# One step of a hybrid sparse-attention and linear-attention trunk: the order of the first loads, splits and products is changed

## The chip, the cores and the metric

The kernel runs on one core of one Trainium2 chip. The metric is device microseconds of one execution. Times of the kernel before are the median of three runs; the profile is of a further execution, taken by the hardware profiler.

The engines are called as in the profile: PE is TensorE (PEld its weight loads), DVE is VectorE, ACT is ScalarE, POOL is GpSimd, SP is SyncE, which issues most of the transfers (DMA).

## What is computed

One inference step of a decoder layer for 1024 prompt tokens and 64 sample tokens (8 sequences of 8 tokens). All 1088 tokens pass through the same weights:

```python
z = split_projection(x @ w_in)          # 13 parts: q_a, k_a, v_a, q_i, k_i, w_i, q_b, k_b, v_b, g_b, a_b, gate_a, gate_b
attn = attend(q_a, k_a, v_a, q_i, k_i, w_i)      # branch A
# log-decay from a_b, chunked gated linear attention over q_b, k_b, v_b  -> o_b   # branch B
merged = sigmoid(gate_a) * (attn @ w_attn_o) + sigmoid(gate_b) * (o_b @ w_gla_o)
mix = merged @ w_out
h = layer_norm(ALPHA * x + mix)
y = layer_norm(ALPHA * h + square(relu(h @ w_ff1)) @ w_ff2)
```

Branch A chooses for every query the 256 keys with the highest indexer score, which is the sum over 8 heads of w_i times relu(q_i . k_i), and attends to those alone. The prompt's keys are its own tokens; a sample's keys are 4096 cached ones, found through a page table, and its own 8 tokens. The model width is 1024, the hidden width 4096.

## The kernel before, in words

**Layout.** Activations stand feature-major: x is eight tiles of 128 features by 1088 tokens. Tokens are cut into three chunks, `CH` (line 36): 384, 384 and 320. Every operand of a large product is split into two parts of type fp32r, a rounded high part and the rest (for x: `xh` and `xl`; for weights: `wh` and `wl`), and a product is three matmuls for each of the eight blocks of 128 inputs: high by high, high by low, low by high (`mm3`, line 620; `fmajor`, line 629, for one weight tile and one token chunk). So one weight tile and one chunk take 24 matmuls, one weight tile and all tokens 72. The matmuls write to one of eight banks; ACT and DVE read the bank.

**Two builds and a planner.** The kernel is built twice. In the first build the uses of every buffer are counted. In the second, a model of the engines' times (class `Clock`, line 97, with a cost for every instruction and a landing time for every transfer) decides in which order the instructions are issued: work is written as generators ("streams", line 262), each of which yields what it has to wait for, and `Order.run` (line 299) takes the first stream in its list whose operands are ready by the model. On the chip each engine executes its own list in exactly this order and waits at an instruction whose operands aren't there. PE's list is common to all streams. The planner also decides whether DVE or POOL makes a low part (`sub`, line 406).

**Jobs.** The stream `main` (line 1701) goes through a list of jobs, one weight tile each. Job 0 is misc (its 128 columns hold k_i, w_i and a_b), job 1 qi0, the first of four tiles with two of the eight q_i heads each; then come the other qi tiles, ka, va, qa, the projections of branch B, the gates, and after them the products with w_attn_o, w_gla_o and w_out. The second half of the kernel (`back`) holds the MLP. `w_get(i)` (line 451) hands out the weight tile of job i, and sees to it that the tile of the next job is split (`w_split`, line 440: ACT makes the high part, DVE or POOL the low part) and that the one behind that is loaded (`w_load`, line 430).

**The start.** SP first issues the loads of the page table, spread over all partitions (`ptab`, line 424), and of a small table of page rows (`ptg`, line 426); then the weight of misc in one load of 0.5 MB (line 468); then x, chunk by chunk, in loads of two feature blocks (line 476), with the weight of qi0 behind the first chunk (line 478). POOL makes the identity matrix `idf` (line 361). DVE works out the row numbers for the gather of cached indexer keys, `ix_i` from ptg and `ix_k` from ptab (lines 496 to 499). Then ACT and DVE split x (lines 533 to 538: an activation and a subtraction for each feature block and chunk); between the first and the second block of the first chunk stands the split of misc's weight (line 540).

**misc and qi0.** `misc_job` (line 668) multiplies the three chunks in turn. After each, ACT copies the whole result to `misc`, and ACT and DVE write the parts that other streams use (`kkh`, `kkl`: the indexer keys; `as3`: the decay input). Behind the third chunk, k_i goes to the output `kidxT` through SP (line 682). `qi_job` (line 658) multiplies its three chunks and splits them into stacks (`to_stacks`, line 645). The stream `wtok_job` (line 687) waits until misc is done, and turns w_i with eight small transposes (`pw`); the streams of the indexer start behind it. `idx_sample` has one more small product there (`pww`).

**What else is named below.** `pages_in_order` (line 514) takes gathered cache rows (`cig`, 16 gathers by POOL) and stores them to DRAM (`ci_s`), from where `idx_sample` loads them again (`kir`) when the gathers are through and the indexer of the prompt has come to its last head. The streams `top_first`, `top_second` and `top_sample` search the threshold of the 256th key bit by bit; a step of `top_sample` (line 1047) is two counts on ACT (`jka`), a small product on PE that adds them for pairs of partitions (`ppr`), and three small operations on DVE (`gs_m`, `gs_u`, `gs_f`). Behind the other two searches DVE makes the masks (`fin`, line 955).

Of the kernel before, what the change touches and what calls it, by code (L numbers as in the profile page):

```python
# [12 lines left out]
F32 = mybir.dt.float32  # L13
F32R = mybir.dt.float32r
# [3 lines left out]
AF = mybir.ActivationFunctionType  # L18
OP = mybir.AluOpType
# [4 lines left out]
P = 128  # L24
# [3 lines left out]
KT = 8  # L28
# [7 lines left out]
CH = ((0, 384), (384, 384), (768, 320))  # L36
# [42 lines left out]
M_SC = 1.0  # L79
M_SD = 0.5  # L80
NGATE = 4
WLATE = 4.0


def f32(ap):
    return ap.bitcast(F32)


def view(ap, offset, dims):
    return bass.AP(tensor=ap.tensor, offset=ap.offset + offset, ap=[list(d) for d in dims])  # L90
# [6 lines left out]
class Clock:  # L97
# [67 lines left out]
    def bank(self, tile):  # L165
        name = tile.tensor.name
        self.psum.add(name)
        free = [i for i in range(8) if self.banks[i] is None or self.banks[i] not in self.pinned]
        i = min(free, key=lambda i: self.used.get(self.banks[i], 0.0))
        self.after[name] = self.used.get(self.banks[i], 0.0)  # L170
        self.banks[i] = name
# [203 lines left out]
def front(ph, tc, env, A, O):  # L375
    nc = tc.nc
    clock = env["clock"]
    pe, dve, act, pool, sp = env["eng"]
    bank, unpin, const, idf = env["bank"], env["unpin"], env["const"], env["idf"]
# [9 lines left out]
    def page(name, dt=F32, shape=None):  # L389
        return clock.take(pgs.tile(shape or [P, T], dt, name=name, tag="pg", bufs=NPG), name, "pg", NPG)  # L390
# [30 lines left out]


    ptab = page("ptab", I32, [P, 8, 32])
    sp.dma_start(ptab, view(A["page_table"], 0, [[0, P], [32, 8], [1, 32]]))
    ptg = cst("ptg", [P, 2], I32)
    sp.dma_start(ptg, A["page_rows"])
    jobs = []
    wt = {}

    def w_load(i):  # L430
        src, kt, m = jobs[i][0]
        pages = []
        for k0 in range(0, kt, 1024 // m):
            kn = min(1024 // m, kt - k0)
            r = page(f"wr{i}_{k0}", F32, [P, kn, m])
            sp.dma_start(r, src[:, k0:k0 + kn, :])
            pages.append([r, None, kn])
        wt[i] = pages

    def w_split(i):  # L440
        for n, e in enumerate(wt[i]):
            r = e[0]
            h = page(f"wh{i}_{n}", F32R, list(r.shape))
            l = page(f"wl{i}_{n}", F32R, list(r.shape))
            act.activation(h, r, AF.Copy)
            sub(l, r, f32(h), WLATE if 1 < state["job"] < mix_at - 1 else 0.0)
            e[0], e[1] = h, l

    state = {"dma": 0, "split": 0, "job": 0}

    def w_get(i):
        while state["split"] <= min(i + (i not in env["alone"]), len(jobs) - 1):
            while state["dma"] <= min(state["split"] + (1 if i < env["deep"] else 2), len(jobs) - 1):
                w_load(state["dma"])
                state["dma"] += 1
            w_split(state["split"])
            state["split"] += 1
        hs, ls = [], []
        for h, l, kn in wt.pop(i):
            for k in range(kn):  # L460
                hs.append(h[:, k, :])
                ls.append(l[:, k, :])
        return hs, ls
# [2 lines left out]
    jobs.append([(W1[4], 8, P), None, None])  # L466
    jobs.append([(W1[0], 8, P), None, None])
    w_load(0)
    state["dma"] = 1
    xh = [env["xpage"](f"xh{k}", F32R, (P, T)) for k in range(KT)]  # L470
    xl = [page(f"xl{k}", F32R) for k in range(KT)]
    xr = {}
    for c, (c0, n) in enumerate(CH):
        for k in range(0, KT, 2):
            xr[k, c] = page(f"xr{k}{c}", F32, [P, 2, 384])
            sp.dma_start(xr[k, c][:, :, :n], A["xT"][k:k + 2, :, c0:c0 + n].rearrange("k p t -> p k t"))
        if c == 0:
            w_load(1)
            state["dma"] = 2


    pid = const("pid", [P, 1], I32)
# [10 lines left out]


    ix_i = cst("ix_i", [P, 8, 2], I32)
    for g in range(8):
        dve.tensor_scalar(ix_i[:, g], ptg, 8.0, float(g), op0=OP.mult, op1=OP.add)
    ix_k = const("ix_k", [1, 256], I32)
    dve.tensor_scalar(ix_k, ptab[0:1].rearrange("p a b -> p (a b)"), 128.0, None, op0=OP.mult)

# [27 lines left out]
                     view(ci_s[p // 2], (p % 2 * 64 + qq * 16) * 8192, [[P, P], [16384, 8], [1, P]]))  # L530


    for c, (c0, n) in enumerate(CH):
        for k in range(KT):
            s = slice(c0, c0 + n)
            r = xr[k - k % 2, c][:, k % 2, :n]
            act.activation(xh[k][:, s], r, AF.Copy)
            dve.tensor_sub(xl[k][:, s], r, f32(xh[k][:, s]))
            if c == 0 and k == 0:
                w_split(0)  # L540
                state["split"] = 1

    def iota_f(name, shape, pattern, base=0):
        n = int(np.prod(shape))
# [84 lines left out]
    def fmajor(w, c, name):  # L629

        c0, n = CH[c]
        ps = bank(name, True)
        yield from mm3(ps[:, :n], w[0], w[1], [x[:, c0:c0 + n] for x in xh], [x[:, c0:c0 + n] for x in xl])
        unpin(ps)
        return ps
# [9 lines left out]
    def to_stacks(ps, c, st):  # L645

        c0, n = CH[c]
        for e in range(2):
            own, oth = slice(e * 64, e * 64 + 64), slice(64 - e * 64, 128 - e * 64)
            act.activation(st[e][own, c0:c0 + n], ps[own, :n], AF.Copy)  # L650
        for e in range(2):
            own, oth = slice(e * 64, e * 64 + 64), slice(64 - e * 64, 128 - e * 64)
            dve.tensor_sub(st[e][oth, c0:c0 + n], ps[own, :n], f32(st[e][own, c0:c0 + n]))

    qis = {}
# [10 lines left out]
        return run  # L666

    def misc_job(w):
        for c in range(3):
            c0, n = CH[c]  # L670
            ps = yield from fmajor(w, c, f"misc{c}")
            act.activation(misc[:, c0:c0 + n], ps[:, :n], AF.Copy)
            for e in range(2):
                act.activation(kkh[e * 64:e * 64 + 64, c0:c0 + n], ps[0:64, :n], AF.Copy)
            for r in (64, 32):
                act.activation(as3[r:r + 16, c0:c0 + n], ps[64:80, :n], AF.Copy)
            for e in range(2):
                dve.tensor_sub(kkl[e * 64:e * 64 + 64, c0:c0 + n], ps[0:64, :n], f32(kkh[0:64, c0:c0 + n]))
            dve.tensor_sub(as3[0:16, c0:c0 + n], ps[64:80, :n], f32(as3[64:80, c0:c0 + n]))
        act.activation(kkn[:, 0], f32(kkh[:, TP:T]), AF.Copy)  # L680
        act.activation(kkn[:, 1], f32(kkl[:, TP:T]), AF.Copy)
        sp.dma_start(O["kidxT"], misc[0:64])
        flags.add("misc")

    flags = set()
# [1015 lines left out]
    def main():  # L1701
        for i in range(len(jobs)):
            state["job"] = i
            if i == project_at - 1:
                x_load(0)
            if i == mix_at - BLEAD:
                gp_load(0)
                branch_load(0)
                gp_load(1)
                branch_load(1)  # L1710
            if jobs[i][2]:
                yield jobs[i][2]
            yield from jobs[i][1](w_get(i))
        while late:
            late.popleft()()

# [739 lines left out]
```

## Time and profile before

| | us |
|---|---|
| median of three runs | 2098.71 (2098.24 to 2099.25) |
| the profiled execution | 2093.24 |
| its span | 2091.5 |
| PE busy | 2032.9 (97%) |
| PEld busy | 1958.7 (94%) |
| DVE busy | 1263.2 (60%) |
| ACT busy | 1120.0 (54%) |
| POOL busy | 761.5 (36%) |

The mean granted clock of PE is 0.988 of full speed, and the transfers move 264.50 MB, 126 GB/s in the mean. A line of the order of time begins with start and length in us; at its end, in square brackets, stands how long the engine had been idle before it, and what ended that. Nearly all instructions are issued through a helper, so that they have one line number (256); they are told apart by the names of their tiles, output first: `misc<-xh,wh` is a matmul that writes a bank of misc from the high parts of x and the weight. A view of waits gives, for each pair of waiting and releasing work, the microseconds in total, the number of times and the longest. A view by stretches gives for each stretch its length, then busy time and number of instructions of PE, PEld, DVE, ACT and POOL, the mean granted clock, the busy share of the DMA engines and GB/s.

### The profile page before, as it was taken

Reading aid. Unit: us, or ns where it says so; the run is one execution under the profiler, and the core shown is the slowest. Engines: PE = TensorE matmul, PEld = TensorE weight load, DVE = VectorE, ACT = ScalarE, POOL = GpSimd, SP = SyncE. Lnnn points to the kernel's source line nnn. Section 1 sums busy time; section 2 is a strip of 40 time slices with the busy share of each in tenths; the row PEclk is TensorE's granted clock in tenths of the full one; section 3 lists DMA queues with packets and bytes.
Section 4 is the critical chain, followed back from the end, with each engine's and each line's share of the span. In section 5 each row is a group of like instructions: output and inputs, shape, how many; then the busy total and the mean of one; then the engine's idle time right before and its main releaser. Section 6 shows DMA issues by size and latency. Waiting matters only on the chain.

```text
span 2091.5 us, 34541 instructions
## 1 busy us (share of the span) xinstructions
PE 2032.9 (97%) x12423; PEld 1958.7 (94%) x12423; DVE 1263.2 (60%) x2633; ACT 1120.0 (54%) x2220; POOL 761.5 (36%) x567
## 2 busy tenths in 40 slices
PE   7999999999799999999999999999999999999997
PEld 7989999898789999989999899999999999999996
DVE  6977777756845675753167755566554444466635
ACT  5687767787567755673024334445343232445543
POOL 3244121222321113113044335565655343364452
PEclk9999999999899999999999999999999999999998
DMA  7674311212023224255573234655523443145542
GB/s 243 254 210 119 124 29 56 82 48 78 27 81 115 83 84 155 68 160 171 190 258 124 69 103 138 182 167 146 159 91 107 124 139 100 61 136 163 186 149 79
DMA packets 185595, 264.50 MB, mean 126 GB/s; under 512 B 22208, under 2 KB 119488, under 8 KB 185424
## 3 DMA queue, kind: packets, MB, share of 16 engines
q1 hardware_dynamic: 177872, 236.87, 35.0%
q0 software_dynamic: 7552, 25.43, 3.9%
q8 instruction: 98, 1.61, 0.3%
q14 instruction: 73, 0.60, 0.1%
HBM read 212.72 MB, written 49.51 MB: 125 GB/s over the span
## 4 chain that ended last, share of the span: by engine, by line
PE 89%; DVE 4%; issue 3%; ACT 2%; POOL 1%; DMA 1%; SPq 0%; ACTq 0%; POOLq 0%; DVEq 0%
PE pf L256 33%; PE gate L256 9%; PE gb L256 4%; PE pwo L256 4%; PE psv L256 4%; PE pmb L256 4%; PE qb L256 2%; PE kb L256 2%; PE qi L256 2%; PE psc L256 2%; PE qa L256 2%; PE po L256 2%; PE pma L256 2%; PE psq L256 2%; PE pov L256 2%
## 5 line engine op out<-in xcount | busy, mean ns | idle before, releaser
L256 PE MATMUL pf<-a,w 128*128 128x384 f32 (+1 forms) x2304 | 397.9, 329 | 2.2 <-POOL a L256 1.3
L256 PE MATMUL pf<-h,w 128*128 128x384 f32 (+1 forms) x2304 | 394.0, 327 | 3.0 <-POOL w L256 1.7
L256 PEld LDWEIGHTS pf<-a,w 128*128 128x128 f32 x2304 | 379.1, 188 | 6.5 <-POOL a L256 1.8
L256 PEld LDWEIGHTS pf<-h,w 128*128 128x128 f32 x2304 | 378.5, 188 | 5.6 <-POOL w L256 2.1
L256 POOL TENSOR_TENSOR wl<-wr,wh 128x1024 fp32r<-128x1024 f32 (+1 forms) x66 | 150.3, 2279 | 467.9 <-ACT wh L256 412.8
L256 POOL TENSOR_TENSOR w<-wr,w 128x512 fp32r<-128x512 f32 x137 | 195.1, 1432 | 132.3 <-ACT w L256 122.2
L256 ACT ACTIVATE w<-wr 128x512 fp32r<-128x512 f32 x272 | 156.5, 618 | 62.7 <-PE pf L256 26.4
L256 DVE TENSOR_TENSOR w<-wr,w 128x512 fp32r<-128x512 f32 x135 | 140.6, 1051 | 52.7 <-ACT w L256 50.2
L256 DVE TENSOR_TENSOR acc<-acc,pf 128x384 f32<-128x384 f32 (+1 forms) x136 | 72.9, 538 | 99.1 <-PE pf L256 98.8
L256 PE MATMUL gate<-xh,wh 128*128 128x384 f32 (+1 forms) x384 | 129.9, 338 | 0.0
L256 PE MATMUL gate<-xh,wl 128*128 128x384 f32 (+1 forms) x384 | 125.5, 327 | 0.0
L256 PE MATMUL gate<-xl,wh 128*128 128x384 f32 (+1 forms) x384 | 125.5, 327 | 0.0
L256 POOL TENSOR_TENSOR a<-fr,a 128x384 fp32r<-128x384 f32 (+1 forms) x54 | 52.6, 975 | 194.5 <-ACT a L256 190.3
L256 ACT ACTIVATE wh<-wr 128x1024 fp32r<-128x1024 f32 (+1 forms) x75 | 74.4, 1005 | 76.2 <-DMA wr<-wgo 39.2
L256 ACT ACTIVATE fr<-pf 128x384 f32<-128x384 f32 (+1 forms) x96 | 44.9, 467 | 113.6 <-PE pf L256 112.6
L256 DVE TENSOR_TENSOR fr<-fr,pf 128x384 f32<-128x384 f32 (+1 forms) x96 | 50.8, 529 | 90.7 <-ACT fr L256 90.5
L256 ACT ACTIVATE a<-fr 128x384 fp32r<-128x384 f32 (+1 forms) x96 | 48.7, 507 | 81.1 <-DVE fr L256 81.1
L256 DVE TENSOR_SCALAR_CACHE_REDUCE jk<-sc,ga_f 128x1024 int8<-128x1024 f32 (+2 forms) x96 | 88.4, 921 | 2.1
L256 ACT ACTIVATE jkb<-sc,gb_f 128x896 int8<-128x896 f32 (+2 forms) x96 | 86.0, 896 | 4.3 <-DVE gb_f L256 2.7
L256 DVE TENSOR_TENSOR phl<-ppt,phl 128x512 fp32r<-128x512 f32 (+1 forms) x80 | 50.2, 636 | 60.4 <-ACT phl L256 59.9
L256 PE MATMUL psv<-wh,xh 128*128 128x256 f32 (+1 forms) x288 | 83.9, 291 | 0.0
L256 PE MATMUL psv<-wl,xh 128*128 128x256 f32 (+1 forms) x288 | 81.2, 282 | 0.0
(487 smaller groups left out, 5158.1 us busy)
## 6 DMA issues: line engine op xcount, KB each, us to landing
wr<-wff SPq DMA_DIRECT2D x256, 256.0 KB
wr<-w SPq DMA_DIRECT2D x43, 512.0 KB
ckr<-kT SPq DMA_DIRECT2D x256, 64.0 KB
ga_s<-gate SPq DMA_DIRECT2D x16, 544.0 KB
ci_s<-cig SPq DMA_DIRECT2D x16, 512.0 KB
kir<-ci_s SPq DMA_DIRECT2D x16, 512.0 KB
wr<-wout SPq DMA_DIRECT2D x13, 512.0 KB
mgp<-ga_s SPq DMA_DIRECT2D x16, 384.0 KB
```

Source lines behind the costliest of these rows:

```text
L256: r = f(*a, **k)
```

## The change

It concerns the first loads, the splits of the first two weights and of x, and the order of the first two jobs.

- The weight of misc is loaded first, in two halves, each ahead of a piece of x's first chunk; the weight of qi0 follows the first chunk as before; ptg comes behind that, and ptab behind all of x.
- 28 transposes of the identity into a bank that nobody reads are put at the head of PE's list.
- The two halves of misc's weight are split by ACT and DVE ahead of the feature blocks 0 and 4 of the first chunk; qi0's weight is split by ACT and DVE behind the first chunk, and `ix_i` is worked out there; `ix_k` comes behind all splits of x.
- `misc_job` multiplies misc and qi0 in the order misc chunk 0, qi0 chunk 0, misc chunk 1, qi0 chunk 1, misc chunk 2, qi0 chunk 2; `main` passes over job 1. The output kidxT is sent ahead of qi0's last chunk; the flag for which `wtok_job` waits is set behind it. `w_get(1)`, which loads the weights of the next two jobs and splits the first of them, is called behind qi0's first chunk.

```diff
@@ front @@
     ptab = page("ptab", I32, [P, 8, 32])
-    sp.dma_start(ptab, view(A["page_table"], 0, [[0, P], [32, 8], [1, 32]]))
     ptg = cst("ptg", [P, 2], I32)
-    sp.dma_start(ptg, A["page_rows"])
@@ w_load @@
-            sp.dma_start(r, src[:, k0:k0 + kn, :])
+            if i > 1:
+                sp.dma_start(r, src[:, k0:k0 + kn, :])
@@ front @@
     w_load(0)
-    state["dma"] = 1
+    w_load(1)
+    state["dma"] = 2
...
-    for c, (c0, n) in enumerate(CH):
+    w0, src0 = wt[0][0][0], jobs[0][0][0]
+
+    def x_in(k, c):
+        c0, n = CH[c]
+        xr[k, c] = page(f"xr{k}{c}", F32, [P, 2, 384])
+        sp.dma_start(xr[k, c][:, :, :n], A["xT"][k:k + 2, :, c0:c0 + n].rearrange("k p t -> p k t"))
+
+    for k in range(0, KT, 2):
+        if k < 4:
+            sp.dma_start(w0[:, 2 * k:2 * k + 4], src0[:, 2 * k:2 * k + 4, :])
+        x_in(k, 0)
+    sp.dma_start(wt[1][0][0], jobs[1][0][0])
+    sp.dma_start(ptg, A["page_rows"])
+    for c in (1, 2):
         for k in range(0, KT, 2):
-            xr[k, c] = page(f"xr{k}{c}", F32, [P, 2, 384])
-            sp.dma_start(xr[k, c][:, :, :n], A["xT"][k:k + 2, :, c0:c0 + n].rearrange("k p t -> p k t"))
-        if c == 0:
-            w_load(1)
-            state["dma"] = 2
+            x_in(k, c)
+    sp.dma_start(ptab, view(A["page_table"], 0, [[0, P], [32, 8], [1, 32]]))
...
-    for g in range(8):
-        dve.tensor_scalar(ix_i[:, g], ptg, 8.0, float(g), op0=OP.mult, op1=OP.add)
     ix_k = const("ix_k", [1, 256], I32)
-    dve.tensor_scalar(ix_k, ptab[0:1].rearrange("p a b -> p (a b)"), 128.0, None, op0=OP.mult)
...
+    def halves(i):
+        r = wt[i][0][0]
+        h = page(f"wh{i}_0", F32R, list(r.shape))
+        l = page(f"wl{i}_0", F32R, list(r.shape))
+        wt[i][0][:2] = h, l
+        return h, l, r
+
+    warm = bank("warm")
+    for _ in range(WARM):
+        pe.transpose(warm[:, :P], idf, idf)
+    wtop, wnext = halves(0), halves(1)
     for c, (c0, n) in enumerate(CH):
         for k in range(KT):
+            if c == 0 and k in (0, 4):
+                h, l, r = (x[:, k:k + 4] for x in wtop)
+                act.activation(h, r, AF.Copy)
+                dve.tensor_sub(l, r, f32(h))
             s = slice(c0, c0 + n)
             r = xr[k - k % 2, c][:, k % 2, :n]
             act.activation(xh[k][:, s], r, AF.Copy)
             dve.tensor_sub(xl[k][:, s], r, f32(xh[k][:, s]))
-            if c == 0 and k == 0:
-                w_split(0)
-                state["split"] = 1
+        if c == 0:
+            h, l, r = wnext
+            act.activation(h, r, AF.Copy)
+            dve.tensor_sub(l, r, f32(h))
+            for g in range(8):
+                dve.tensor_scalar(ix_i[:, g], ptg, 8.0, float(g), op0=OP.mult, op1=OP.add)
+    dve.tensor_scalar(ix_k, ptab[0:1].rearrange("p a b -> p (a b)"), 128.0, None, op0=OP.mult)
+    state["split"] = 2
@@ misc_job @@
     def misc_job(w):
+        (h, l, kn), = wt[1]
+        q = [h[:, k, :] for k in range(kn)], [l[:, k, :] for k in range(kn)]
+        st = [page(f"qi{e}", F32R) for e in range(2)]
         for c in range(3):
             c0, n = CH[c]
+            if c:
+                ps = yield from fmajor(q, c - 1, f"qi0_{c - 1}")
+                to_stacks(ps, c - 1, st)
+            if c == 1:
+                w_get(1)
             ps = yield from fmajor(w, c, f"misc{c}")
...
         sp.dma_start(O["kidxT"], misc[0:64])
+        ps = yield from fmajor(q, 2, "qi0_2")
+        to_stacks(ps, 2, st)
+        qis.update(enumerate(st))
         flags.add("misc")
@@ main @@
-            yield from jobs[i][1](w_get(i))
+            if i != 1:
+                yield from jobs[i][1](w_get(i))
```

`WARM` is 28.

More of the change, by code (lines that the diff above doesn't have):

```diff
@@ L81 @@
 NGATE = 4
+WARM = 28
 WLATE = 4.0
```

## The prediction

> **What bounds the kernel now.** I read the page's head first, then TensorE's waits, then the order of time of the first 45 us.
>
> ```profile
> span 2091.5 us, 34541 instructions
> PE 2032.9 (97%) x12423; PEld 1958.7 (94%) x12423; DVE 1263.2 (60%) x2633; ACT 1120.0 (54%) x2220; POOL 761.5 (36%) x567
> ```
>
> TensorE (PE) is busy 97% of the span: its work decides the time, and what can be gained without removing products are the 58.6 us (2091.5 - 2032.9) in which it stands, and stretches in which its products run slowly. All but a few of the changed lines act before 45 us. There PE's waits are:
>
> ```profile
> PE misc L256 <- ACT wh L256: 9.0, 1, 9.0
> PE misc L256 <- POOL wl L256: 1.4, 1, 1.4
> PE pw L256 <- ACT misc L256: 1.4, 1, 1.4
> PE qi L256 <- DVE wl L256: 1.1, 1, 1.1
> ```
>
> In the order of time (start, length, engine, operation) the same stretch reads:
>
> ```profile
> 0.82 0.40 SPq L256 DMA_DIRECT2D ptab<-page_table  x1
> 1.74 0.44 SPq L256 DMA_DIRECT2D wr<-w  x1
> 2.22 2.11 SPq L256 DMA_DIRECT2D xr<-xT  x4
> 7.51 0.52 ACT L256 ACTIVATE xh<-xr 128x384 fp32r<-128x384 f32 x1 [5.41 <-DMA xr<-xT]
> 7.94 1.04 ACT L256 ACTIVATE wh<-wr 128x1024 fp32r<-128x1024 f32 x1
> 9.04 0.69 PE L256 MATMUL misc<-xh,wh 128*128 128x384 f32 x1 [9.04 <-ACT wh L256]
> 9.07 2.36 POOL L256 TENSOR_TENSOR wl<-wr,wh 128x1024 fp32r<-128x1024 f32 x1 [7.59 <-ACT wh L256]
> 11.96 0.52 PE L256 MATMUL misc<-xh,wh 128*128 128x384 f32 x1
> ...
> 15.44 0.34 PE L256 MATMUL misc<-xh,wl 128*128 128x384 f32 x1
> ...
> 21.33 0.31 PE L256 MATMUL misc<-xh,wh 128*128 128x320 f32 x1
> ...
> 24.84 0.34 PE L256 MATMUL qi<-xh,wh 128*128 128x384 f32 x1
> 25.14 1.22 DVE L256 TENSOR_TENSOR wl<-wr,wh 128x1024 fp32r<-128x1024 f32 x1
> 29.99 0.52 PE L256 MATMUL qi<-xl,wh 128*128 128x384 f32 x1
> ...
> 42.30 0.34 PE L256 MATMUL qi<-xh,wh 128*128 128x384 f32 x1
> ```
>
> Two things are to be seen. First, the waits: PE begins at 9.04, when the weight's high part is there, and stands again for its low part, which GpSimd (POOL) needs 2.36 us for. Second, the pace. From 15.44 to 21.33 34 products of 384 columns start, 0.173 us each; from 21.33 to 24.84 24 of 320 columns, 0.146 us each. But from 11.96 to 15.44 it is 11 of 384 columns, 0.316 us each, and the product at 29.99 has the same length of 0.52 us as these, against 0.34. The view by stretches (busy us of PE, its weight loads, DVE, ACT, POOL, then the granted clock) has the reason for the latter:
>
> ```profile
> 25.00:30.00 5.00, 2.59 (x17) 1.91 (x16) 4.26 (x8) 4.84 (x12) 0.00 (x0) 0.90 0.01 2
> 30.00:35.00 5.00, 5.00 (x23) 4.68 (x23) 2.83 (x6) 2.46 (x6) 1.87 (x1) 0.76 0.93 300
> ```
>
> The granted clock is 0.90 and 0.76 there, where PE was busy for only 2.59 of the first 5 us. At half the clock that makes 1.0 and 2.4 us (0.10 and 0.24 of 5, twice), and half of these 3.4 us, 1.7, is lost. PE's start has the same slow pace.
>
> The first two input products (misc, then qi0) with the small pw and pww end at 42.30, where qi1 starts. At full pace they are 96 x 0.173 + 48 x 0.146 = 23.6 us, and about 1.3 us for pw and pww. So of the first 42.3 us some 17.4 are waits and slow products.
>
> **The change, part by part.** The chain of waits (start, length, what) names the arrivals:
>
> ```profile
> 4.37 7.52 DMA wr<-w
> 11.90 10.37 DMA xr<-xT
> ```
>
> *Loads.* The second weight is there at 11.89. Ahead of it are the page table (128 x 1 KB, 0.13 MB), the first weight (0.52 MB) and the first chunk of x (four of 0.39 MB). The page table goes to the end, and the first big load is issued at 0.82 instead of 1.74. The second weight follows with 0.13 MB less ahead, 0.35 us at 0.39 MB per us (the 1.70 MB that landed between 7.51 and 11.89): it lands at 11.89 - 0.92 - 0.35 = 10.6. If the queue and not the issue sets the pace, only the 0.35 us is gained and it lands at 11.5. The halved load adds one issue, 0.44 us of SP, inside the 0.92 already counted as free before the data run.
>
> A rule speaks against halving: the Trainium skill (DMA: Bandwidth & Descriptors, Anatomy of one DMA) gives each transfer a fixed cost of about 2.0 us beside its bytes. As an estimate by that page the additional transfer would make the sum 2.0 us worse if transfers ran one after another. The four x loads above leave SP within 2.11 us, so several are under way at once here, and I charge nothing.
>
> *First product.* Its first half weight and first x piece have 0.66 MB to come instead of 1.05 MB, so the 7.51 becomes about 5.6 (0.92 and 1.0 us earlier), and PE starts at about 6. Its end doesn't depend on that: the last x piece of the chunk lands just ahead of the second weight, some 1.35 us (0.52 MB), at 9.2; two activations of 0.52 and a subtraction of 0.54 (the row below) later the last operand is there, at 10.8. 24 products at 0.173 from 6 fit in between; at 0.316 they end at 13.6 (a rival below).
>
> *Split on DVE.* POOL's 2.36 us go; two halves on ACT and DVE come, together 1.04 and 1.22 us. They lie between arrivals of x. A tile's view (shortest, median, longest ns, first and last start) shows a side gain:
>
> ```profile
> L256 DVE TENSOR_TENSOR xl<-xr,xh x24: 473/542/2416, 8.1 to 23.2; 128x384 fp32r<-128x384 f32 x16, 128x320 fp32r<-128x320 f32 x8
> ```
>
> The longest subtraction of x, 2.42 us against a median of 0.54, is the one beside POOL's weight split; that goes. The eight ix_i and the ix_k on DVE wait for their tables now, with the x subtractions of later chunks queued behind ix_i: 1 us, hidden by the product of qi0, which PE does next from the first chunk alone. The first gather moves from 12.8 to about 14:
>
> ```profile
> L256 SPq DMA_DIRECT2D ci_s<-cig x16: 319/320/1637, 30.5 to 79.9; - x16
> L256 SPq DMA_DIRECT2D kir<-ci_s x16: 360/1244/2582, 111.3 to 176.6; - x16
> ```
>
> Its data are stored until 79.9 and read from 111.3, so 1 us costs nothing; with the cover gone it would cost that 1 us. SP gets the next two weights behind x and ahead of the output kidxT, for which it has to wait for misc's last chunk; that costs nothing and lets these weights come sooner.
>
> *Alternation.* This sets the sum. After the first product PE needs the second weight: landed 10.6, its high part 1.04 us later, its low part another 1.22, with hand-overs 13.0. By then 26 of the 144 products are done. What is left is 70 x 0.173 + 48 x 0.146 = 19.1 us, with no arrival late: before, all second-chunk activations had ended by 18.75 (the row of 12 below), so its last subtraction comes by 19.3, and PE, which starts that chunk at 16.8, asks for its last operands at 20.5. The third chunk has landed by 21.0 (22.27 less 1.27), and PE comes to it at 25.1. So the products end at 32.1, and pw and pww at 33.4. pw waited 1.4 us for ACT before; what is late next is ACT again:
>
> ```profile
> 12.96 5.79 ACT L256 ACTIVATE xh<-xr 128x384 fp32r<-128x384 f32 x12 [1.09 <-DMA xr<-xT]
> ...
> 23.98 0.47 ACT L256 ACTIVATE misc<-misc 128x384 f32<-128x384 f32 x1
> 26.34 0.49 ACT L256 ACTIVATE misc<-misc 128x384 f32<-128x384 f32 x1
> 39.56 1.98 ACT L256 ACTIVATE qi<-qi 64x384 fp32r<-64x384 f32 x4
> ```
>
> One chunk of misc takes ACT 2.36 us, two chunks of qi0 1.98. ACT is through with x at about 21.9 (21.0 and two activations). Two chunks of misc, two of qi0 and one weight of 1.04 later it is 29.7; the third chunk's copy, all that pw needs, is done by 30.2, and PE asks at 32.1. So that wait goes, and a lack of 1.9 us would bring it back.
>
> *Transposes.* The identity is there at 1.39:
>
> ```profile
> 1.10 0.29 POOL masks.py:199 TENSOR_SCALAR_AFFINE_SELECT idf<-idf 128x128 f32<-128x128 f32 x1
> 278.00 0.60 PE L256 MATMUL pskt<-idf,gk 128*128 128x128 f32 x4
> 278.35 0.42 PE L256 MATMUL qb<-xh,wh 128*128 128x384 f32 x1
> ```
>
> Four such transposes pass in 0.35 us, 0.09 each, or 0.18 at the slow pace. 28 end between 4.0 and 6.5 us; at worst they delay the first product by 0.5 us, which the late x pieces hide. What they can give is the pace, and there the row is against a full gain: between 6 and 13 us PE has 26 products, 4.5 us of work in 7, and two waits near 1 us for the second weight. The row 25.00:30.00 shows the clock falling at a share of 0.52, and that cost 1.7 us.
>
> The Trainium skill (TensorE: Matmul & The Clock Gate, Part 1) says that the clock halves after an idle window of about 3.4 us. By that rule no wait here is long enough, and the stage ends at 33.4. The trace disagrees: between 11.96 and 29.99 no wait was over 1.4 us, and the clock fell.
>
> **Sum.** 42.30 - 33.4 = 8.9 us with the clock kept, 7.2 with one slow stretch, 6.3 if the second weight gains only 0.35 us too. I take 8.1, between the first two, because PE's share of work (0.64) lies a little above that of the row (0.52). Everything later is the same work in a kernel whose PE is busy 97%, so it moves up. The profiled execution took 2093.24 us for its span of 2091.5; it becomes 2085.1. The median of the runs is 5.47 above it, and I add the same: 2098.7 - 8.1 = 2090.6.
>
> **Rivals.** The order of PE's later work comes from the planner, whose times the change shifts, and PE can't pass an instruction that waits. One place shows what that costs:
>
> ```profile
> PE ppr L256 <- ACT jka L256: 11.5, 2, 8.5
> 525.00:530.00 5.00, 5.00 (x35) 4.30 (x34) 2.03 (x4) 3.39 (x9) 0.00 (x0) 1.00 0.02 3
> ...
> 545.00:555.00 10.00, 7.08 (x42) 6.83 (x41) 9.62 (x19) 7.52 (x16) 0.57 (x1) 0.83 0.01 2
> 555.00:565.00 10.00, 3.56 (x22) 3.21 (x20) 9.69 (x18) 0.95 (x2) 5.12 (x3) 0.82 0.00 0
> ...
> 564.47 1.15 ACT L256 ACTIVATE jka<-ssa,gs_f 128x1024 int8<-128x1024 f32 x1 [9.05 <-DVE gs_f L256]
> ```
>
> PE stood twice, for 11.5 us, at a search step's pair sum (ppr), because ACT's count waited 9.05 us for a DVE that was filled with mask work (9.62 and 9.69 of 10 us). The clock fell both times (0.83, 0.82); at 1.7 us each the place is worth 14.9 us.
>
> A, the gain ends there: DVE's work does not move up, PE only comes 8.1 us sooner and waits longer. Time 2098.7. For it: DVE is full from 545. Against it: in 525 to 530 DVE worked 2.03 of 5 us, so its masks too began when PE's results let them.
>
> B, slower: the new order puts a second pair sum behind mask work in this way, with the price of this place: 2090.6 + 14.9 = 2105.5. It decides from a wait of 12.3 us on (8.1 + 4.2). For it: the planner did so once; against it: 32 search steps, and only two of them stood long.
>
> C, the transposes don't do what they are for: the first product runs at 0.316 to 13.6, which puts off the two products of qi0 that would fill the wait (0.6 + 0.35 us), and the clock comes 3.4 us later, half of it lost, 1.7. The gain falls by 2.6 to 6.3: 2092.4. For it: PE's gaps between 6 and 13; against it: the first start needed the 3.5 us from 11.96 to 15.44 to get fast, and 28 slow transposes (5 us) give such a run.
>
> **How the numbers follow.** 0.2% of the time, 4.2 us, is about what a measurement of this kernel can tell from no change. The forecast has 0.60, C 0.08, both faster by more: 0.68. A has 0.16, same; B 0.16, slower. The front alone gives 2089.8 to 2092.4; later order can take half of that one place (7.4) off, so the range begins at 2083, and it reaches 2104, past A and nearly to B.
>
> **What would show it.** Right: PE's first product near 6 us; no wait of misc for a low part; a wait near 1 us of qi for its weight at 12 to 13; no wait of pw; qi1 starting near 33.4 (32.5 to 36); PE's waits after that adding up as before, the largest at ppr. Wrong: the second weight landing after 12; pace 0.316 beyond 17 us; qi1 after 37; or, with qi1 at 33.4, a ppr, psc or pwo wait that is longer by the 8 us gained.

## The result, and the profile after

| | before | after |
|---|---|---|
| median | 2098.98 us (2098.24 to 2099.32, 4 runs) | 2109.27 us (2108.43 to 2110.21, 4 runs) |
| ratio after to before | | 1.0055, 95% interval 1.0043 to 1.0067 |
| the profiled execution, its span | 2093.24, 2091.5 us | 2110.21, 2108.5 us |

The change makes the kernel slower by 10.3 us; the prediction said 8.1 us faster (2090.6 us, within 2083 to 2104). The head of the page after:

```profile
span 2108.5 us, 34601 instructions
PE 2045.6 (97%) x12451; PEld 1965.8 (93%) x12451; DVE 1250.0 (59%) x2631; ACT 1123.1 (53%) x2222; POOL 769.1 (36%) x569
```

TensorE has the 28 transposes more, nothing else, and is busy for 12.7 us longer than before (2045.6 against 2032.9): 5.1 of these are the transposes; as no product was added, the rest is time by which products ran longer. The head tells nothing of where. The order of time of the start does (start, length, engine, operation, and in brackets the idle time before it with what ended that):

```profile
1.45 5.11 PE L257 MATMUL warm<-idf 128*128 128x128 f32 x28 [1.45 <-POOL idf masks.py:199]
...
32.51 0.31 PE L257 MATMUL qi<-xh,wl 128*128 128x320 f32 x1
32.75 0.35 PE L257 MATMUL pw<-idf,misc 8*128 8x8 f32 x3
34.87 0.35 PE L257 MATMUL pw<-idf,misc 8*128 8x8 f32 x3 [1.76 <-ACT misc L257]
38.18 0.38 PE L257 MATMUL pw<-idf,misc 8*128 8x8 f32 x2 [2.97 <-ACT misc L257]
38.49 0.69 PE L257 MATMUL qi<-xh,wh 128*128 128x384 f32 x1
```

Up to 32.5 us all is as forecast: the transposes end at 6.6, the first product starts at 6.3, qi0 waits 0.64 us for its weight's low part, and the products of the two jobs end at 32.5 (forecast 32.1). Then pw stands twice, 4.7 us together. It waits for ACT's copies of misc. ACT's own rows say why they are late, and SP's and POOL's rows why ACT is:

```profile
33.24 1.06 ACT L257 ACTIVATE wh<-wr 128x1024 fp32r<-128x1024 f32 x1 [8.92 <-DMA wr<-w]
34.32 0.49 ACT L257 ACTIVATE misc<-misc 128x384 f32<-128x384 f32 x1
...
37.69 0.44 ACT L257 ACTIVATE misc<-misc 128x320 f32<-128x320 f32 x1
```

```profile
12.11 0.34 SPq L257 DMA_DIRECT2D ptab<-page_table  x1
20.48 5.27 SPq L257 DMA_DIRECT2D ci_s<-cig  x2
25.84 1.12 SPq L257 DMA_DIRECT2D wr<-w  x2
```

In the kernel before, SP's rows read:

```profile
12.96 0.34 SPq L256 DMA_DIRECT2D wr<-w  x1
...
30.45 2.11 SPq L256 DMA_DIRECT2D ci_s<-cig  x2
```

And after, POOL's:

```profile
13.70 1.22 POOL L257 DMA_INDIRECT cig<-ciT,ix_i  x1 [11.09 <-DVE ix_i L257]
15.22 6.54 POOL L257 DMA_INDIRECT cig<-ciT,ix_i  x1 [0.30 <-issue]
```

Read from POOL upwards: the gathers start at 13.70 and their second issue takes 6.54 us. SP has the stores of these two gathers in its list ahead of the weights of jobs 2 and 3, so these weights are issued at 25.84; before, the next weight left SP at 12.96, ahead of the first stores. ACT has the split of that weight in its list ahead of the copies of misc, and stands at it for 8.92 us. PE stands at pw. The view by stretches (columns as in the prediction) shows what follows on the clock:

```profile
30.00:35.00 5.00, 3.24 (x25) 2.96 (x24) 0.00 (x0) 1.74 (x3) 0.62 (x1) 1.00 1.02 413
35.00:40.00 5.00, 2.03 (x10) 1.91 (x10) 2.84 (x6) 4.83 (x12) 4.54 (x4) 0.60 0.45 136
40.00:45.00 5.00, 5.00 (x22) 4.50 (x21) 3.74 (x9) 2.02 (x6) 1.28 (x2) 0.72 0.94 317
```

The granted clock falls to 0.60 and 0.72, and the first 12 products of qi1 start some 0.32 us apart instead of 0.173.

The rest of the loss lies later. To follow it, I take from both traces the time at which a kernel has the same amount of PE work still to do (every product counted at the median length of its kind), and subtract before's time. A negative number is a lead. The columns are before's times; the other rows are the experiments below.

| kernel | 38 us | 63 | 129 | 236 | 458 | 600 | 842 | 1013 |
|---|---|---|---|---|---|---|---|---|
| after | -8.6 | -0.9 | -0.9 | +4.9 | +13.7 | +3.1 | +4.0 | +14.3 |
| e1, after in before's order | -9.2 | -9.0 | -4.7 | -4.8 | -4.8 | -4.1 | -4.2 | -4.1 |
| e2, before in after's order | -2.8 | -2.4 | -3.4 | +1.7 | +11.6 | +1.3 | +2.0 | +11.0 |
| e3, weights ahead of stores | -9.5 | -7.8 | -7.7 | -1.8 | +7.3 | -3.1 | -2.2 | +6.3 |
| e5, e1 without transposes | -7.9 | -7.7 | -2.4 | -2.4 | -2.4 | -2.2 | -2.2 | -2.1 |
| e6, own order to 210 us | -8.2 | 0.0 | +0.3 | +5.3 | +5.4 | +4.8 | +4.8 | +4.8 |
| e7, own order from 635 us | -9.1 | -8.7 | -4.6 | -4.6 | -4.6 | -4.3 | -3.6 | +6.9 |
| e8, own order to 650 us | -9.1 | -1.6 | -1.7 | +4.4 | +13.3 | +2.7 | +9.3 | +9.1 |
| e9, before, LAG 0.29 | +1.1 | +2.8 | +7.0 | +7.0 | +10.4 | +14.4 | +15.3 | +14.0 |
| e11, after, LAG 0.29 | -8.6 | -1.3 | +2.7 | +2.6 | +6.0 | +9.8 | +10.5 | +9.4 |

The lead of 8.6 us is lost in four steps: 7.7 at pw; 5.8 in the indexer (130 to 170 us); 8.8 at 450 to 465, which come back by 600, where before's own long waits for the pair sum ppr are gone; and 10.2 in the attention between 842 and 1013. The table ends there because before's profiled execution is 5.7 us below before's median: what single profiles show behind it is not compared, the ends are compared by medians. The last column stands 1.6 to 8.3 us above what the ratios below give for the same kernel, always to the same side, so the table tells where something is lost, and the ratios tell how much.

In the step at 450 PE waits at a pair sum, as in the prediction's rivals but at another place. First the waits of PE in the whole of after (us, times, longest), then its stretches:

```profile
PE ppr L257 <- ACT jka L257: 8.5, 3, 6.1
PE pw L257 <- ACT misc L257: 4.7, 2, 3.0
```

```profile
450.00:460.00 10.00, 5.65 (x38) 5.08 (x36) 9.08 (x28) 9.94 (x18) 0.00 (x0) 0.96 0.00 0
460.00:470.00 10.00, 7.82 (x37) 7.69 (x38) 5.07 (x15) 8.21 (x18) 2.37 (x1) 0.70 0.00 0
```

ACT itself is full there (9.94 of 10 us); in the prediction's place it stood and waited for DVE.

### The profile page after: what moved, and what is told of

Same layout as the page of the kernel before. It is cut to its first block, busy times and chain, and to the rows that moved or that the text cites. A ratio compares the mean times of both kernels' runs of the same rounds, so it can differ in the third digit from the quotient of the medians.

```text
span 2108.5 us, 34601 instructions
## 1 busy us (share of the span) xinstructions
PE 2045.6 (97%) x12451; PEld 1965.8 (93%) x12451; DVE 1250.0 (59%) x2631; ACT 1123.1 (53%) x2222; POOL 769.1 (36%) x569
## 4 chain that ended last, share of the span: by engine, by line
PE 85%; DVE 6%; issue 4%; ACT 3%; DMA 1%; POOL 1%; SPq 0%; ACTq 0%; DVEq 0%; POOLq 0%
PE pf L257 33%; PE gate L257 8%; PE gb L257 4%; PE psv L257 4%; PE pmb L257 4%; PE pwo L257 4%; PE kb L257 2%; PE qb L257 2%; PE psc L257 2%; PE po L257 2%; PE qi L257 2%; PE pma L257 2%; PE psq L257 2%; PE qa L257 1%; PE pob L257 1%
```

## The experiments

Three theories stood after this. **O**: the changed start is worth its 8 to 9 us, and what is lost comes from the new order of the instructions that the planner found around it. **S**: of this, 7 us come from the two stores ahead of the weights. **C**: the attention begins 14 us later in the new order (its first product at 653.5 us instead of 639.1), and by its end the gates' products, which PE does between the attention's steps, are used up; that is the loss behind 842. The rival of O is that the changed start itself takes from later work (DVE or a transfer that doesn't move up).

The runs were made in three groups with a median of before for each: 2098.42 us for e1 to e4, 2100.64 for e5 to e8, 2100.76 for e9 to e12. So kernels of different groups are compared by their ratios to before, and a ratio is turned into us with 2099.

For the runs in a borrowed order the planner's decisions of a kernel (which stream comes next, which engine makes a low part) were written down and played back in the other kernel:

```diff
 while not all(s.done for s in list(until)):
+    if PLAN and (self.left or self.held):
...
+        i = self.left.popleft()
...
+        s.step()
...
-if clock.t["pool"] + 0.0021 * n < clock.t["dve"] + 0.00104 * n + late:
+if clock.plan.side("f", out, clock.t["pool"] + 0.0021 * n < clock.t["dve"] + 0.00104 * n + late):
```

In the traces PE's products in e1 come in before's order from the 155th on to the end, those in e2 in after's order from the 121st on (the transposes not counted).

**e1: the changed kernel, all decisions from the kernel before.**

> The changed kernel, but every choice of the planner (which stream goes next, which engine makes a low part) is taken from the kernel before; only the first two products, their loads and splits stand as the change has them. Theory O (the edits gain 8 to 9 us in the first 31 us, and the loss comes from the order that the planner then chose): 2089 to 2094 us, the lead over the kernel before still 6 to 9 us at qi1 and at the end, and no wait of pw over 1 us. Theory D (the edits themselves harm what follows, whatever the order, by holding pages and banks or by feeding the indexer later): above 2100 us.

Measured: 2092.86 us (2090.38 to 2094.1), before 2098.42; ratio 0.9973 (0.9964 to 0.9983). With the old order the change is a gain of 5.7 us (0.27% of 2099). The lead is 9.0 us at 63 us and 4.7 from 129 on. So O holds, with less at the end than the 6 to 9 us that it expected, and its rival has a part of its own: 4.3 us of the lead are taken back between 63 and 130. The rows of SP, of DVE and the stretches of e1 show where:

```profile
59.82 14.68 SPq L330 DMA_DIRECT2D ci_s<-cig  x6
...
76.34 0.48 SPq L330 DMA_DIRECT2D gn<-gla_norm_g  x1
```

```profile
80.55 0.17 DVE L330 TENSOR_SCALAR gn<-gn 128x2 f32<-128x2 f32 x1 [1.53 <-DMA gn<-gla_norm_g]
...
109.49 5.95 DVE L330 SCALAR_TENSOR_TENSOR sc<-r,wtok,sc 128x384 f32<-128x384 f32 x10
115.36 1.21 DVE L330 TENSOR_TENSOR kir<-kir,kih 128x1024 fp32r<-128x1024 f32 x1
```

```profile
115.00:120.00 5.00, 3.38 (x12) 3.10 (x13) 4.81 (x9) 4.70 (x10) 3.60 (x2) 0.78 0.49 144
120.00:125.00 5.00, 5.00 (x27) 4.91 (x26) 4.88 (x12) 4.05 (x7) 2.40 (x1) 0.88 0.75 297
```

From the row of gn on DVE works without a gap, and PE waits 2.0 us for the last of these rows (before: 1.3) and at 86 to 88 us 0.8 for another row of DVE and 0.3 for ACT. After the wait of 2.0 us the granted clock is 0.78 and 0.88; in before it stays at 1.00 there. The rival A of the prediction, work of DVE that does not move up, is found here and not at the pair sum: there e1 waits as before:

```profile
PE ppr L330 <- ACT jka L330: 11.5, 2, 8.6
PE pss L330 <- DVE kir L330: 2.0, 1, 2.0
```

The full stretch of DVE begins late because of a load. In before the row of gn stands at 86.67, behind a wait of 2.00 us for the same load:

```profile
86.67 0.24 DVE L256 TENSOR_SCALAR gn<-gn 128x2 f32<-128x2 f32 x1 [2.00 <-DMA gn<-gla_norm_g]
```

So it moves up by 6.1 us, not by 9.0. SP issues that load at 76.34 (before: 82.01) behind six stores that wait for gathers. That is the queue of S once more, at another place; it was read from the rows, not tried alone.

**e2: the kernel before, all decisions from the changed one.**

> The kernel before with the planner's choices taken from the changed kernel. Theory O: the later losses of the changed kernel (18.3 us from the 46th us on) without its early lead: about 2115 to 2119 us. Theory D: within 4 us of the kernel before, 2095 to 2103 us.

Measured: 2106.76 us (2106.19 to 2107.26); ratio 1.0041 (1.0027 to 1.0055). The order alone, without any of the change, costs 8.6 us. It is less than the 2115 to 2119 us that O expected. The 18.3 us of that expectation fit the two profiled spans, which lie 17.0 us apart, and the lead that was left at 46 us; the medians lie 10.3 apart. And in this order the old start itself gains some 3 us (qi1 at 39.30 instead of 42.30), without a wait at pw: the next weight leaves SP at 12.3 us. The table shows the same steps as after at 129 to 236, at 458 and behind 842; from 63 to 1013 us it has e2 lose 13.4 us and after 15.2.

**e3: the changed kernel in its own order, only the loads of the weights of jobs 2 and 3 stand ahead of the first two stores in SP's list.**

```diff
...
+    for i in (2, 3):
+        soon[i] = page(f"wr{i}_0", F32, [P, 8, P])
+        sp.dma_start(soon[i], W1[i - 1])
     sp.dma_start(ptab, view(A["page_table"], 0, [[0, P], [32, 8], [1, 32]]))
```

> The changed kernel in its own order, and of all instructions only two move: the loads of the weights of jobs 2 and 3 are issued behind x, ahead of the first two stores of gathered rows. Theory S (the 8.9 us for which ACT waited for that weight, with SP standing at a store whose gather had not landed, cost the early lead): ACT's wait is under 1 us, pw doesn't wait, qi1 starts at about 33.5 us instead of 38.5 and at full pace, and of the 7.3 us lost there 5 to 7 are still there at the end: 2102 to 2104 us. Rival: later waits swallow it, 2107 to 2110 us.

Measured: 2102.67 us (2101.23 to 2104.61); ratio 1.0022 (1.0012 to 1.0032), 0.0033 or 6.9 us below after (uncertain by some 3). PE's products come in after's order from the first to the last. Its order of time (SP, ACT, PE):

```profile
11.48 1.40 SPq L330 DMA_DIRECT2D wr<-w  x2
...
22.34 9.81 SPq L330 DMA_DIRECT2D ci_s<-cig  x4
```

```profile
23.72 1.06 ACT L330 ACTIVATE wh<-wr 128x1024 fp32r<-128x1024 f32 x1
24.81 0.49 ACT L330 ACTIVATE misc<-misc 128x384 f32<-128x384 f32 x1
```

```profile
32.15 0.66 PE L330 MATMUL pw<-idf,misc 8*128 8x8 f32 x8
32.74 0.45 PE L330 MATMUL qi<-xh,wh 128*128 128x384 f32 x1
33.03 0.34 PE L330 MATMUL qi<-xl,wh 128*128 128x384 f32 x1
```

No wait at pw, qi1 at 32.74 at full pace, and the 6.9 us stay to the end. S is shown: two places in SP's list are worth that. This is also the start that the prediction described.

**e4: the kernel before, one constant of the planner changed.** LAG is the delay that the planner's model puts between the end of an instruction and the one that waits for it; nothing but the order, and which engine makes a low part, hangs on it.

```diff
-LAG = 0.3
+LAG = 0.32
```

> The kernel before, one constant of the planner changed (the lag that it adds behind every instruction, 0.30 to 0.32 us), so that nothing changes but the order in which it issues the same instructions. Theory O needs that the order alone moves the time by about 10 us: 2099 to 2120 us, with other waits of PE than before. If the order hardly matters: 2097 to 2101 us.

Measured: 2124.87 us (2122.24 to 2127.21); ratio 1.0126 (1.0109 to 1.0143). That is beyond the 2120 us that was expected at most: an order that nothing in the kernel called for is worth 26 us, three times the whole lead.

**e5: e1 without the 28 transposes** (`WARM = 0`).

> As e1 (the changed kernel with the choices of the kernel before), without the 28 transposes of the identity; nothing else differs. Theory W (they bring the clock up before the first product): the products of misc's first chunk start 0.32 us apart up to about 10 us, and qi1 starts later than in e1 by the 1 to 2.6 us that the prediction gave for a slow start: 2094 to 2096 us. Rival (the late x pieces and the wait for qi0's weight hide a slow start): qi1 within 0.5 us of e1, 2092 to 2094 us.

Measured: 2093.66 us (2092.39 to 2095.11), before 2100.64 on that chip; ratio 0.9969 (0.9957 to 0.998), the same as e1. The transposes bring the pace that they are for, as e5 without them shows:

```profile
5.43 0.69 PE L330 MATMUL misc<-xh,wh 128*128 128x384 f32 x1 [5.43 <-ACT xh L330]
...
12.92 0.52 PE L330 MATMUL misc<-xl,wh 128*128 128x384 f32 x1
13.24 0.45 PE L330 MATMUL misc<-xh,wl 128*128 128x384 f32 x1
13.52 0.34 PE L330 MATMUL misc<-xh,wh 128*128 128x384 f32 x1
```

Products start 0.32 us apart until 13.2, and the first chunk's last one at 13.87; with transposes (e1) they are 0.173 apart nearly from the start, and it is at 11.87. Of these 2.0 us 0.4 go because qi0 then waits for its weight, qi1 starts at 34.51 instead of 33.16, as W expected, and at 63 us e5 is 1.3 us behind e1. In the ratios nothing of it is to be seen, so that the transposes gain time is not shown, and neither is the 2.6 us that the prediction put on their failing.

**e6, e7, e8: the changed kernel with its own order in one part and before's in the rest.** e6 has its own order for the first 419 steps of the streams (to about 210 us) and then before's; e8 changes over at the attention's beginning (at 650 us in PE's rows); e7 has before's order up to the attention and its own from there (635 us in PE's rows).

> The changed kernel; in the planner's own order until both indexers are through (419 of its 2265 steps, about 210 us), from there in the order of the kernel before. Theory P (each place costs by itself): at 220 us PE is 5 to 6 us behind the kernel before, as in the changed kernel, and stays so: 2103 to 2106 us. Rival (a bad start makes the rest bad as well): 2109 us or more.

> The changed kernel; in the order of the kernel before until attention is let in (1274 steps, about 625 us), from there in the planner's own. Theory C (the 8 to 10 us at 930 to 960 us come from attention starting 14 us later while gate products, its cover, were used up 11 us sooner): attention starts at 633 to 638 us and PE's waits of pov, ppt and psq add up to 3 to 6 us, as in the kernel before; 2091 to 2096 us. Rival (the own order within attention is at fault): 8 to 10 us lost at 930 to 960 us, 2100 us or more.

> The changed kernel; in the planner's own order until attention is let in (1290 steps, about 640 us), from there in the order of the kernel before. Theory C: attention starts at 650 to 655 us with the gate products of the first steps used up, and at the end of attention PE waits 7 us or more longer than the kernel before, though the order there is that kernel's: 2107 to 2112 us. Rival: no additional loss behind 640 us, 2101 to 2104 us.

Measured: e6 2102.01 us (2100.69 to 2104.26), ratio 1.0009 (0.9999 to 1.0019). e7 2101.69 (2099.25 to 2103.77), ratio 1.0004 (0.9995 to 1.0014). e8 2107.69 (2106.15 to 2109.19), ratio 1.0035 (1.0022 to 1.0047). Taken as steps from before's order to the changed kernel's own: the start in before's order -5.7 us (e1), its own order to 210 us +7.6 (e6 less e1), to 650 us +5.5 (e8 less e6), behind it +4.2 (after less e8), together +11.5 (by the ratio; 10.3 by the medians). Each step is uncertain by some 3 us, and the last two contain what the change of order in e8 costs at the place where it is made: 6.6 us are lost there between 600 and 842, of which PE waits 3.1 for loads of kar, and neither after nor before lose as much. For e6 the trace shows what theory P expected (5.3 us behind at 236, 4.8 at 1013); its time is 1 us below P's range.

e7 does not settle C. The lead is still 3.6 us at 842, and then 10.5 us are lost, but the attention's first product stands at 645.8 us, not at the 633 to 638 that were expected (e1: 634.9): it is late here too. e8 speaks against C as I had put it: its attention begins late (649.8 us), and behind 842 nothing is lost. Its time lies in the range that C gave, but not for C's reason. What decides behind 842 is how the order mixes gates and attention. The last gate product starts at 932.3 in before and at 931.0 in after. The attention's products behind it, first in before, then in after (shortest, median, longest ns, first and last start):

```profile
L256 PE MATMUL psq<-kar,qq x6: 221/274/277, 932.4 to 933.7; 128*128 128x128 f32 x6
L256 PE MATMUL ppt<-idf,pp x8: 272/372/422, 933.8 to 942.4; 128*128 128x128 f32 x8
L256 PE MATMUL pov<-phl,vpr x12: 278/386/582, 932.8 to 948.0; 128*128 128x256 f32 x12
```

```profile
L257 PE MATMUL psq<-kar,qq x16: 220/282/561, 932.1 to 946.6; 128*128 128x256 f32 x8, 128*128 128x128 f32 x8
L257 PE MATMUL ppt<-idf,pp x24: 270/366/421, 932.6 to 955.1; 128*128 128x128 f32 x24
L257 PE MATMUL pov<-phl,vpr x32: 278/283/583, 931.2 to 959.6; 128*128 128x256 f32 x32
```

26 are left in before, 72 in after. They form chains through ACT and DVE with nothing for PE to do in between, as the stretches of after show:

```profile
930.00:940.00 10.00, 7.21 (x43) 6.25 (x41) 5.45 (x24) 7.46 (x21) 0.72 (x1) 0.85 0.79 274
940.00:950.00 10.00, 5.19 (x28) 3.60 (x28) 5.51 (x27) 7.31 (x22) 1.45 (x2) 0.84 0.63 214
950.00:960.00 10.00, 7.38 (x31) 6.81 (x32) 7.56 (x18) 8.84 (x24) 2.46 (x3) 0.62 0.13 33
```

Counted in the same way, with what the lead changes by from 842 to 1013:

| | before | e1 | e5 | e6 | e8 | after | e2 | e3 | e7 | e4 | e9 | e10 | e11 | e12 |
|---|---|---|---|---|---|---|---|---|---|---|---|---|---|---|
| attention products behind the last gate product | 26 | 26 | 26 | 26 | 26 | 72 | 72 | 72 | 72 | 104 | 12 | 12 | 12 | 0 |
| lost, us | 0 | 0.1 | 0.1 | 0.0 | -0.2 | 10.2 | 9.0 | 8.5 | 10.5 | 12.3 | -1.2 | 0.3 | -1.1 | -4.0 |

Each kernel with 72 left loses 8.5 to 10.5 us, with the old start (e2) as with the new; these four share one order there. e4, in another order, has 104 left and loses 12.3. In e9, e10 and e11 the attention begins at 668.9, 653.9 and 664.2 us, later than in before (639.1), and with 12 left they lose nothing. So C loses its first half (because the attention begins late). Its second half (the cover is used up) goes with the losses in all these traces; no run changed the number of products left alone.

**e9 to e12: both kernels with LAG 0.29 and 0.31.** They ask whether before's order was an ordinary one.

> The kernel before with one planner constant changed (LAG, the delay that the planner's model sets between an instruction's end and who waits for it, 0.30 to 0.29): the same instructions in another order. Theory L (a lottery): beyond the first 45 us a new order is worth anything within some 12 us either way of the kernel before, whatever caused it, with no change of the start; expected 2090 to 2112. Rival T (the kernel before's order is nothing special, and only the changed start draws a bad one): within 3 us of the kernel before. The start (qi1 at 42.3 us) stays as before in both.

> The same with LAG 0.31. Theory L: anywhere from 2090 to 2120, and not between the kernel before and the 26 us slower one at 0.32 by rule. Rival T: within 3 us of the kernel before. A third view, D (the order gets worse smoothly as the constant grows): half of the 26 us, 2110 to 2114.

> The changed kernel with LAG 0.29. Its queue of SP again has two stores of gathered rows ahead of the weights of jobs 2 and 3, so the wait of pw of about 4.7 us and the slow clock behind it must be there again (lead of 9 us at 31 us, 1 to 2 us at 46). Theory L: the rest is drawn anew; time 2090 to 2115, and the losses in the indexer, at the pair sums and in the attention lie at other places or have other sizes than in the changed kernel. Rival T (the changed start draws a bad order by itself): the same losses at the same places, 2106 to 2112.

> The changed kernel with LAG 0.31. The wait of pw again, 4 to 5 us. Theory L: 2090 to 2115, losses elsewhere. Rival T: 2106 to 2112 with the losses at the same places. If both kernels' times over the constant overlap, the change's own worth in its own orders can't be told from two single orders.

| LAG | before | after |
|---|---|---|
| 0.29 | 1.0027 (1.0018 to 1.0036), 2106.3 us | 1.0015 (1.0006 to 1.0024), 2102.87 us |
| 0.30 | 1 | 1.0055 (1.0043 to 1.0067) |
| 0.31 | 1.005 (1.0037 to 1.0064), 2110.93 us | 1.0552 (1.0538 to 1.0567), 2217.4 us |
| 0.32 | 1.0126 (1.0109 to 1.0143) | not run |

T falls: before at 0.29 and 0.31 is 5.7 and 10.5 us slower, so its order at 0.30 is the best of the four that were run. The start, which was expected to stay, moved by some 1 us: qi1 stands at 43.44 and 41.60 us. D fits 0.31 and 0.32 but not 0.29. L holds in kind, and its size was far too small: e12 is 116 us slower than before, where 2115 us was the end of L's range. Its largest wait, and a row of PE from the middle of it:

```profile
PE ppr L257 <- ACT jka L257: 103.9, 18, 22.6
```

```profile
341.99 0.58 PE L257 MATMUL ppr<-gs_p,pm 128*128 128x2 f32 x2 [4.80 <-ACT jka L257]
```

```profile
340.00:350.00 10.00, 1.17 (x4) 1.00 (x4) 9.21 (x32) 9.80 (x19) 0.00 (x0) 0.50 0.00 1
```

Step after step of the search has its pair sum in PE's list with no product between: PE works 1.17 of 10 us. This is the prediction's rival B, PE standing at ppr, at many times its size, in an order that a change of 0.01 in a constant brings up. The reason is not B's: ACT is full with the counts (9.80 of 10 us) and does not wait for masks.

e9 and e11 are the fairest pair: at the same constant both kernels wait at the same later places (psv 7.8 us, ppr 6.0 us), and there the change is a gain of 2.5 us by the ratios (0.0012; their intervals overlap) and 3.4 by the medians, with the wait at pw still in it (2.3 and 2.8 us). With overlapping intervals that gain is not shown.

## Why the prediction was wrong, point by point

- **Loads, first product, split, alternation, transposes: right.** The first product starts at 6.3 (forecast about 6), qi0 waits 0.64 us for its weight, the products end at 32.5 (32.1), and where nothing else interferes qi1 starts at 32.74 (e3; 33.4). The lead at 38 us is 8.2 to 9.5 in the starts with transposes, against 8.9 for a kept clock; the 8.1 that I took lay below, because I charged half a slow stretch that did not come. The longest subtraction of x is 0.56 us, so the 2.42 went as said. C, the rival of failing transposes, did not happen.
- **"So that wait goes": wrong, worth 7 us.** The step added up ACT's work and left out what each piece waits for. It moved the split of the next weight with that weight's load, and for the load it said: "SP gets the next two weights behind x and ahead of the output kidxT … that costs nothing and lets these weights come sooner". They are ahead of kidxT, but behind two stores that wait for gathers, and came 12.9 us later (25.84 against 12.96). What the step missed in the code is that `w_get(0)` loaded and split ahead before, and now finds job 1 split, so that the next loads hang on `w_get(1)` behind qi0's first chunk; by then the stream of the gathers has its stores in SP's list. The text gave the point from which the wait returns, a lack of 1.9 us; ACT stood 8.92.
- **The clock at that wait.** The waits of 1.76 and 2.97 us, with 0.7 us of work between them, brought the granted clock to 0.60. By the Trainium skill (TensorE: Matmul & The Clock Gate, Part 1) the clock halves after an idle window of about 3.4 us; neither wait is that long, the two with the small products between them are, and this trace can't tell which of these counts.
- **"Everything later is the same work in a kernel whose PE is busy 97%, so it moves up": wrong, and the larger part.** It is the same work in another order. e2 has the order without the change (+8.6 us), e1 the change without the order (-5.7 us). Even with the old order only 5.7 of the 9 us arrive: between 80 and 125 us DVE is full, from a row on whose load moved up by only 6.1 us, and the clock falls once more (0.78).
- **The rivals.** A named DVE, at 545 us; the pair sums there moved up with the rest (e1), and DVE took its share at 80 to 125, behind a load. B named the right kind of event and one instruction for it, ppr: in after, ppr costs PE less than before (8.5 us against 11.5), and the order put its losses at pw, in the indexer and behind the last gate product; at LAG 0.31 it is ppr. B's chance of 0.16 rested on "32 search steps, and only two of them stood long". That counted places in one order, which the planner had made with one value of a constant; it says little on the next order.
- **The range** ended at 2104 us, and 2109.3 lies outside. For a new order it had one place, B's, with a time of 2105.5, and it ended short of that; the other orders of the unchanged kernel (e4, e9, e10) lie 5.7 to 26 us above it.

How much each of the later losses is worth by itself stays open. Open, too, is why the planner, with this start, leaves 72 attention products behind the last gate product; its decisions were played back, not taken apart. Each of the losses of the indexer (130 to 170 us) was seen only as part of an order, not tried alone.

## What to carry to other kernels

Where a program orders the instructions, a change of the start is two changes, and the second can be larger: play the old order back around the new code before judging either. e1, the new start in the old order, at 0.9973 of before is faster than both kernels, and so is e5 without the transposes. When a load is moved, follow its engine's list up to the first entry that waits for something else, and then the lists of those who wait for the load: three lists in a row (SP, ACT, PE) turned two stores into 7 us.

## What the runs showed of the hardware

- The pace at the start is 0.32 us for a product of 384 columns until PE has worked for some us: from 11.48 to 15.2 in before (3.7 us), from 8.32 to 13.2 in e5 (4.9 us, the first two steps wider than 0.32). The transposes show the same turn by their own distance: 0.213 us from 1.45 to 5.2, then 0.109 (after and e1, 3.7 us; in e3 the turn comes at 6.0, 4.5 us). The clock column shows 1.00 in all these stretches; at the start only the distance of the products tells the pace.
- An indirect gather's issue takes POOL about 1.0 us, and 5.7 to 6.5 us for one of the 16 in the changed starts (1.3 at most in before). It lies at 15 us, while x is still landing; but x lands as well in before and e2, where the gathers at 12 to 20 us take 0.9 to 1.3. The reason is open.
- With PE at work for 1.17 of 10 us the granted clock was 0.50 for as long as that lasted (340 to 370 us in e12).
